# VectorE in place of GpSimd in the planned parts of a two-layer diffusion step, and the recurrence's constants computed first

## The chip, the cores and the metric

One core of a Trainium2 chip runs the whole program in one launch. The metric is the device time of that launch in microseconds (us). The engines are TensorE (PE, with its weight loads as PEld), VectorE (DVE), ScalarE (ACT), GpSimd (POOL) and SyncE (SP, which here only issues DMAs). Each takes its own instructions strictly in program order; an engine waits for another, or for a DMA, at semaphores.

## The reference

640 tokens (128 of a prompt, 512 of a denoising sample, in one array with features on the partitions) pass through two layers and a final norm:

```python
def trunk(x, cvec, ctx_caches):
    for layer in range(DEPTH):                       # DEPTH = 2
        sh_m, sc_m, gt_m, sh_f, sc_f, gt_f = ada_params(cvec, w_mod[layer], b_mod[layer])
        h = rmsnorm(x, g_mix[layer]) * (1.0 + sc_m) + sh_m
        mix = attn_lru_mixer(h, ...) if layer == 0 else pool_mixer(h, w_pool, s_pool)
        x = x + gt_m * mix
        h = rmsnorm(x, g_ffn[layer]) * (1.0 + sc_f) + sh_f
        x = x + gt_f * peer_ffn(h, ...)
    return rmsnorm(x, g_final), new_state
```

`ada_params` is silu(c) @ w_mod + b_mod. `attn_lru_mixer` is latent attention beside a bidirectional RG-LRU recurrence, whose decay is exp(-8 r softplus(-lam)). `pool_mixer` takes centred window means of widths 2 to 16. `peer_ffn` finds for each token and head the 16 best of 128x128 product keys, gathers those experts' rows and sums them. All is float32.

## The kernel before

A float32 product is made from three passes of TensorE over rounded parts: ACT writes the rounded half (`hh` of an activation, `wh` of a weight), another engine writes the rest (`hl`, `wl`) as a subtraction, and PE multiplies hh by wh, hl by wh and hh by wl. So each normed feature block k (8 of them, 128x640) needs, after the RECIPROCAL of the root mean square, a product with `rt` (L483, `xn`), a scale and shift per trunk (L494 on DVE or L491 on ACT), a rounding on ACT (L498), and the rest (L501). Each weight tile needs L307 on ACT and L316 on DVE or POOL.

The program runs in stages:

- The first plan (span 0 to 80 us): modulation columns of layer 0 (weights streamed by DMA; products L1771 on PE; dot products L1802 on DVE, each 128x1024 with its sum, or L1806 on POOL and the sum on ACT, L1810), the first norm, and the first three chunks of the input projection (L529). Behind it `lru_columns` makes the recurrence's column constants from `lam` (L552 to L565: two activations on ACT and 28 operations of 128x8 on DVE).
- The recurrence's plan (80 to 209), the attention's with the output projection (209 to 376).
- Layer 0's PEER: its norm and first query products are planned (from 377); then top-16 searches (L1202 to L1206 on DVE: ten instructions' worth for each of 16 rows of scores in a chunk) and the gather loops, which are written out by hand.
- Layer 1's pooling mixer (planned, 2021 to 2076), its PEER (norm planned from 2079), and the final norm (planned, from 3724).

A `Plan` is a list of operations with their dependencies and, for each engine that could run them, a time (`dve_pool(n)` gives V or G for an elementwise operation of n columns). `run` tries several hundred orderings of the list with those times, puts each operation on the engine where it ends soonest, and then emits the instructions in the best order found. So the tables set both the engine and the place in each engine's queue. `run(S=1.5)` says that ACT is taken for the first 1.5 us. `take` names a ring of buffers that an operation needs. Outside the plans nothing is chosen: there 11 weight rests of each PEER layer (L316) are on POOL, and so are the indirect DMA gathers.

Of the kernel before, what the change touches and what calls it, by code (L numbers as in the profile page):

```python
# [11 lines left out]
F32 = mybir.dt.float32  # L12
# [144 lines left out]
def tile_trunk(ctx: ExitStack, tc: tile.TileContext, a, o):  # L157
# [35 lines left out]
    def mod_ops(plan, l, chunks, pool, tmp, late=0.0):  # L193
        done, loads = {}, []
        prev = []
        for n in chunks:
            w = {}

            def load(e, n=n, w=w):
                w[0] = tmp.tile([128, D], F32, name="wm", tag="wm", bufs=2)  # L200
                SP.dma_start(w[0], a[f"w_mod{l}"][n if l else n - 8])

            ld = plan.add({"SP": 0.1}, load, *loads[-1:], take="wm", late=late)
            arrive = plan.add({"dma": 1.5}, lambda e: None, ld)
            loads.append(ld)
            ends = []
            for cc in range(2):
                pr = {}

                def mult(e, n=n, cc=cc, w=w, pr=pr):  # L210
                    if e is V:
                        junk = tmp.tile([128, D], F16, name="mjunk", tag="mjunk", bufs=1)
                        V.scalar_tensor_tensor(junk, w[0], 1.0, silu[:, cc], op0=OP.mult, op1=OP.mult,
                                               accum_out=mcol[:, l, n, cc:cc + 1])
                    else:
                        pr[0] = pool.tile([128, D], F32, name="mp", tag="mp", bufs=1)
                        G.tensor_tensor(pr[0], w[0], silu[:, cc], op=OP.mult)

                def total(e, n=n, cc=cc, pr=pr):
                    if e is S:  # L220
                        S.activation(pr[0], pr[0], AF.Copy, accum_out=mcol[:, l, n, cc:cc + 1])
# [6 lines left out]
                ends.append(t)  # L228
            done[n] = ends
        return done  # L230
# [92 lines left out]
    class Weights:  # L323
# [143 lines left out]
    def dve_pool(n):  # L467
        return {"V": 0.07 + n * 1.04e-3, "G": 0.1 + n * 2.2e-3}

    def norm_ops(plan, tmp, A, B, rdy, cols_rdy, fine=0):  # L470
# [4 lines left out]
        for k in range(KD):  # L475
            t, xs, hs, ends = [], [], [], []
            for c0, c1 in ((0, HT), (HT, T)) if k < fine else ((0, T),):
# [29 lines left out]
                ends.append(plan.add(dve_pool(c1 - c0), rest, r))  # L507
# [59 lines left out]
    def mixer0(p_mm, tmp, gt, firsts):  # L567
# [6 lines left out]
        with tc.tile_pool(name="pz", bufs=1) as pz:  # L574
# [5 lines left out]
            with tc.tile_pool(name="pa", bufs=1) as pa:  # L580
# [7 lines left out]
                with tc.tile_pool(name="plru", bufs=1) as pl:  # L588
# [76 lines left out]
                    def recurrence(d, jj, prev):  # L665
# [10 lines left out]
                        for q in range(2):  # L676
# [53 lines left out]
                            gm = plan.add(dve_pool(T), gated, sg[1])  # L730
                            rs = plan.add({"V": 1.5}, rest, de, take="t", free=(len(plan.ops),))
                            ro = plan.add({"S": 0.65}, root, rs, table="sqrt")
                            sd = plan.add(dve_pool(T), scaled, ro, gm)
                            en = plan.add({"V": 1.05}, scan, sd)
                            if d:
                                en = plan.add(dve_pool(T), both, en)
# [82 lines left out]
                    for j in range(3):  # L819
                        def scaled(e, j=j):  # L820
                            V.scalar_tensor_tensor(cq[:, j], cq[:, j], col("g_q", j), rtq[0],
                                                   op0=OP.mult, op1=OP.mult)
                        n = plan.add({"V": 0.75}, scaled, rq)
                        h = plan.add({"S": 0.65}, lambda e, j=j: S.activation(hh[:, j], cq[:, j], AF.Copy),
                                     n, ops[0])
                        split.append(plan.add(dve_pool(T), lambda e, j=j: e.tensor_tensor(
                            hl[:, j], cq[:, j], hh[:, j], op=OP.subtract), h))
                    kvn = []
                    for j in range(2):
# [7 lines left out]
                        plan.add(dve_pool(NK), lambda e, j=j: e.tensor_tensor(  # L837
# [12 lines left out]
                    for jj in range(2):  # L850
                        for d in range(2):
                            end = recurrence(d, jj, end)
                        for q in range(2):
                            j = 2 * jj + q
                            plan.add(dve_pool(T), lambda e, j=j, jj=jj, q=q: e.tensor_tensor(
                                gug[:, j], gug[:, j], hss[jj][:, q], op=OP.mult), *end, gugd[j])
                    mod_ops(plan, 0, range(16, 24), None, tmp, 1.0)
# [5 lines left out]
                with tc.tile_pool(name="pv_", bufs=1) as pvp, tc.tile_pool(name="ps", bufs=1) as pS:  # L863
# [3 lines left out]
                    plan = Plan(mm=3, s=2, t=4, mp=1, wm=2)  # L867
# [48 lines left out]
                    for j in range(4):  # L916
                        h = plan.add({"S": 0.65}, lambda e, j=j: S.activation(hh[:, 4 + j], gug[:, j],
                                                                              AF.Copy), *ms, late=1.0)
                        gugs.append(plan.add(dve_pool(T), lambda e, j=j: e.tensor_tensor(
# [124 lines left out]
                    done = mod_ops(plan, 0, range(24, 48), pS, tmp)  # L1044
# [16 lines left out]
                    def sum_up(e):  # L1061
                        ssq.accum()
# [6 lines left out]
                    for d in range(KD):  # L1069
# [10 lines left out]
                        if d < KD - 2:  # L1080
                            parts.append(plan.add({"G": 1.5}, sum_up, q, free=(q,)))
# [12 lines left out]
    def mixer1(p_mm, tmp, A, B, gt):  # L1094
        with tc.tile_pool(name="pq", bufs=1) as pq:
# [53 lines left out]
            for k in (7, 6, 5, 4, 3, 2, 1, 0):  # L1149
# [3 lines left out]
                dep = plan.add(dve_pool(T), tt(xt, xT[:, k], rt, OP.mult), *rdy)  # L1153
                dep = plan.add({"S": 1.1}, hidden(k, xt), dep)
                cur, c0, c1 = hp[:, k], 1, HW
                for lev in range(g + 1):
# [7 lines left out]
                    dep = plan.add(dve_pool(HW), f, dep)  # L1164
                    cur = nx
                dep = plan.add({"V": 0.3, "G": 0.6}, edges(cur, g), dep)
                dep = plan.add({"V": 0.9}, centre(k, cur, xt), dep)
                dep = plan.add({"S": 0.8}, lambda e, k=k, xt=xt: S.activation(hh[:, k], xt, AF.Copy), dep)
                split[k] = plan.add(dve_pool(T), tt(hl[:, k], xt, hh[:, k], OP.subtract), dep)
# [503 lines left out]
    with tc.tile_pool(name="tmp", bufs=1) as tmp, tc.tile_pool(name="pmm", bufs=1, space=PSUM) as p_mm:  # L1673
        with tc.tile_pool(name="pm0", bufs=1) as pm0:
            gb, bb = col("g_mix0"), pm0.tile([128, KD], F32, name="bb")
            A, B, gt = mcol[:, 0, 8:16], mcol[:, 0, 0:8], mcol[:, 0, 16:24]
            plan = Plan(t=4, s=2, sq=4, mp=2, wmn=6, wm=6)
# [59 lines left out]
            for k in range(KD):  # L1737
# [12 lines left out]
                if 0 < k < KD - 2:  # L1750
                    sums = [plan.add(dve_pool(T), join, *prev, *sums, free=prev)]
# [13 lines left out]
            for n in range(8):  # L1765
# [30 lines left out]
                for cc in range(2):  # L1796
                    pr = []

                    def mult(e, n=n, cc=cc, pr=pr):
                        if e is V:  # L1800
                            junk = pm0.tile([128, D], F16, name="mjunk", tag="mjunk", bufs=1)
                            V.scalar_tensor_tensor(junk, scale_w[n], 1.0, silu[:, cc], op0=OP.mult,  # L1802
                                                   op1=OP.mult, accum_out=mcol[:, 0, n + 8, cc:cc + 1])
                        else:
                            pr.append(pm0.tile([128, D], F32, name="mp", tag="mp", bufs=2))
                            G.tensor_tensor(pr[0], scale_w[n], silu[:, cc], op=OP.mult)  # L1806

                    def total(e, n=n, cc=cc, pr=pr):
                        if e is S:
                            S.activation(pr[0], pr[0], AF.Copy, accum_out=mcol[:, 0, n + 8, cc:cc + 1])  # L1810

                    m = plan.add({"V": 1.2, "G": 2.4}, mult, sc_d[n][0], *sl[2 * cc:2 * cc + 2], take=("mp", "G"),
                                 free=(sc_d[n][1],) if cc else ())
                    parts.append(plan.add({"S": 0.95}, total, m, free=(m,), skip=(m, "V")))
# [14 lines left out]
            plan.run(S=1.5)  # L1829
            lru_columns(pm0)  # L1830
        mixer0(p_mm, tmp, gt, firsts)
# [8 lines left out]
    with tc.tile_pool(name="tmp", bufs=1) as tmp, tc.tile_pool(name="pmm", bufs=1, space=PSUM) as p_mm:  # L1840
        plan = Plan()
        rdy = reciprocals(plan)
        for k in range(KD):
            for h in range(2):
                y = []

                def product(e, y=y, k=k, c0=h * HT, c1=h * HT + HT):
                    y.append(tmp.tile([128, HT], F32, name="y", tag="y", bufs=16))
                    if e is V:
                        V.scalar_tensor_tensor(y[0], xT[:, k, c0:c1], col("g_final", k), rt[:, c0:c1],  # L1850
                                               op0=OP.mult, op1=OP.mult)
                    else:
                        G.tensor_tensor(y[0], xT[:, k, c0:c1], rt[:, c0:c1], op=OP.mult)

                def scaled(e, y=y, k=k):
                    if e is S:
                        S.activation(y[0], y[0], AF.Copy, scale=col("g_final", k))
# [110 lines left out]
```

## Time and profile before

| | |
|---|---|
| median of 3 runs | 3744.69 us (3743.12 to 3746.17) |
| profiled execution | 3744.72 us, its span 3743.0 us |
| busy share of the span | PE 96%, PEld 80%, DVE 80%, ACT 44%, POOL 22% |
| chain that ended last | PE 40%, DVE 5%, all others under 1% |
| mean granted clock of PE | 0.979 of full speed |

The shares are means over stages with different limits, so stages are read one by one. In the section with rows, a timeline row gives the start, the duration, engine, line, operation, tiles and shape, the count x of like instructions in a row, and in brackets how long the engine was idle before it and who ended that. A group row of the lines view gives line, engine, operation, shapes and count, then the busy time and the mean in ns of one. A row of the waits view gives who waited for whom: us in total, times, longest. A row of the windows view gives the window, its length, and the busy us and instruction count of PE, PEld, DVE, ACT and POOL, the granted clock of PE, the DMA share and GB/s. Durations of successive DVE instructions overlap by some 0.08 us, so the spacing of starts is the time that one costs.

### The profile page before, as it was taken

What the parts mean: (1) busy time and instruction counts of PE and PEld (TensorE: products, weight loads), DVE (VectorE), ACT (ScalarE), POOL (GpSimd) and SP (SyncE); (2) the same over time, 40 slices, a digit from 0 to 9 for tenths busy, and PEclk for the clock granted to TensorE, in tenths of its full rate; (3) what the DMA queues carried; (4) which work ended last, traced back from release to release, by engine and by line L of the source; (5) the groups of instructions that cost most, each with busy time, mean ns of one, the idle gap of its engine ahead of it and who ended that gap; (6) DMA issues with size and microseconds to landing.
All of it is one profiled execution on the core that took longest, in us unless ns stands there. A gap on an engine that the chain in (4) does not pass through costs nothing. (4 is left out here: it accounts for less than half of the span.)

```text
span 3743.0 us, 52891 instructions
## 1 busy us (share of the span) xinstructions
PE 3589.5 (96%) x18190; PEld 2984.0 (80%) x18190; DVE 2996.6 (80%) x6901; ACT 1645.0 (44%) x2900; POOL 836.7 (22%) x673
## 2 busy tenths in 40 slices
PE   7989889999999999999996798999999999999997
PEld 5957788888888888888885797888888888888886
DVE  7877788898988788888887798988989666666665
ACT  3743323756657333333333323657567433333333
POOL 3122311111111422222223320111211312222221
PEclk9999899999999999999998899999999999999998
DMA  5234125888888999999991215878888978988883
GB/s 200 75 110 141 51 65 196 277 264 287 260 264 283 369 311 327 330 330 324 324 320 47 71 57 172 266 261 287 260 271 278 341 257 296 296 296 297 298 297 105
DMA packets 400162, 894.58 MB, mean 239 GB/s; under 512 B 33746, under 2 KB 170386, under 8 KB 399252
## 3 DMA queue, kind: packets, MB, share of 16 engines
q1 hardware_dynamic: 272884, 490.07, 41.0%
q0 software_dynamic: 74016, 271.09, 21.2%
q10 hardware_dynamic: 52992, 130.05, 8.9%
q8 instruction: 142, 2.33, 0.3%
q14 instruction: 128, 1.05, 0.1%
HBM read 758.26 MB, written 132.81 MB: 238 GB/s over the span
## 5 line engine op out<-in xcount | busy, mean ns | idle before, releaser
L316 DVE TENSOR_TENSOR wl<-wr,wh 128x1024 fp32r<-128x1024 f32 x544 | 660.0, 1214 | 517.6 <-ACT wh L307 440.1
L307 ACT ACTIVATE wh<-wr 128x1024 fp32r<-128x1024 f32 (+1 forms) x578 | 601.5, 1042 | 898.4 <-PE po L1631 735.6
L1287 POOL DMA_INDIRECT gat<-in_u_dram,idx x256 | 292.5, 1143 | 1252.8 <-DVE oh L1477 643.3
L1287 POOL DMA_INDIRECT gat<-in_v_dram,idx x256 | 302.7, 1182 | 1019.1 <-DVE accP L1609 957.5
L1631 PE MATMUL po<-wgh,wh 128*128 128x512 f32 x2032 | 501.8, 389 | 0.0
L1631 PE MATMUL po<-wgl,wh 128*128 128x512 f32 x2032 | 501.8, 389 | 0.0
L1631 PE MATMUL po<-wgh,wl 128*128 128x512 f32 x2032 | 501.8, 389 | 0.0
L1631 PEld LDWEIGHTS po<-wgh,wh 128*128 128x128 f32 x2032 | 381.4, 188 | 79.2
L1631 PEld LDWEIGHTS po<-wgl,wh 128*128 128x128 f32 x2032 | 381.4, 188 | 79.2
L1631 PEld LDWEIGHTS po<-wgh,wl 128*128 128x128 f32 x2032 | 381.4, 188 | 79.2
L1410 DVE SCALAR_TENSOR_TENSOR gat<-gat,hP 128x1024 f32<-128x1024 f32 x256 | 310.8, 1218 | 19.9 <-DMA gat<-in_u_dram,idx 19.8
L1609 DVE SCALAR_TENSOR_TENSOR accP<-gat,aP,accP 128x1024 f32<-128x1024 f32 x254 | 324.8, 1279 | 0.5
L1479 DVE TENSOR_SCALAR oh<-iota,ij,gs 128x128 f16<-128x128 f16 x1024 | 320.0, 313 | 0.0
L1418 ACT ACTIVATE oh<-oh,gs 128x128 f16<-128x128 f16 x1024 | 316.8, 387 | 0.0
L1541 ACT ACTIVATE wgh<-w 128x512 fp32r<-128x512 f32 x256 | 161.9, 632 | 207.7 <-PE po L1631 204.4
L1477 DVE TENSOR_SCALAR oh<-iota,ij 128x128 f16<-128x128 f16 x1024 | 251.4, 246 | 0.0
L1543 DVE TENSOR_TENSOR wgl<-w,wgh 128x512 fp32r<-128x512 f32 x256 | 174.8, 683 | 7.8 <-ACT wgh L1541 7.8
L1430 ACT ACTIVATE stag<-pgm 128x512 f32<-128x512 f32 x256 | 135.5, 579 | 0.0
L316 POOL TENSOR_TENSOR wl<-wr,wh 128x1024 fp32r<-128x1024 f32 (+2 forms) x34 | 72.7, 2138 | 276.4 <-ACT wh L307 276.4
L1423 PE MATMUL pgm<-oh 128*128 128x128 f16 x1024 | 129.4, 220 | 0.0
L1424 PE MATMUL pgm<-oh 128*128 128x128 f16 x1024 | 128.1, 219 | 0.0
L189 DVE SCALAR_TENSOR_TENSOR mjunk<-wm,silu 128x1024 f16<-128x1024 f32 x96 | 116.9, 1218 | 12.7 <-DMA gt__12588<-g_d 9.2
(2282 smaller groups left out, 7223.7 us busy)
## 6 DMA issues: line engine op xcount, KB each, us to landing
wr<-in_uT_dram SPq DMA_DIRECT2D x256, 512.0 KB
wr<-in_v_dram SPq DMA_DIRECT2D x256, 512.0 KB
g_d<-stag ACTq DMA_DIRECT2D x128, 512.0 KB
act_d<-at ACTq DMA_DIRECT2D x240, 256.0 KB
at<-act_d SPq DMA_DIRECT2D x240, 256.0 KB
wm<-in_w_mod_dram SPq DMA_DIRECT2D x88, 512.0 KB
hl<-g_d SPq DMA_DIRECT2D x128, 256.0 KB
wr<-in_w_q_dram SPq DMA_DIRECT2D x32, 512.0 KB
```

The lines of the kernel that those rows point to most:

```text
L307: S.activation(hi[:, :n], RAW[i][:, :n], AF.Copy)
L316: (eng or (V if e == "v" else G)).tensor_tensor(lo[:, :n], RAW.pop(i)[:, :n], hi[:, :n], op=OP.subtract)
L1287: G.indirect_dma_start(out=r, out_offset=None, in_=a[f"u{l}" if s < 128 else f"v{l}"], in_offset=bass.IndirectOffsetOnAxis(ap=idx[:, s % 1 ...
L1410: V.scalar_tensor_tensor(ug, ug, 1.0, hP, op0=OP.mult, op1=OP.mult, accum_out=aP[:, s:s + 1])
L1418: S.activation(oh[:, 2], oh[:, 1], AF.Copy, scale=gr[:, tl:tl + 1])
L1430: S.activation(sg[:, :, t4:t4 + 4], pgm.rearrange("p q i -> p i q"), AF.Copy, scale=1.0 / GSCALE)
L1477: V.tensor_scalar(oh[:, 0], iota16, ij[:, 1, tl:tl + 1], None, op0=OP.is_equal)
L1479: V.tensor_scalar(oh[:, 1], iota16, ij[:, 0, tl:tl + 1], gs[:, 0, tl:tl + 1], op0=OP.is_equal, op1=OP.mult)
L1541: S.activation(wh, w32, AF.Copy)
L1543: return lambda: V.tensor_tensor(wl, w32, wh, op=OP.subtract)
L1609: V.scalar_tensor_tensor(accP, vg, aP[:, s:s + 1], accP, op0=OP.mult, op1=OP.add)
L1631: PE.matmul(po[d], (hi, lo)[x][:, d * 128:(d + 1) * 128], (wh, wl)[y], start=(n == 0 and p == 0), stop=False)
```

## The change

In every plan the POOL choice is taken out: weight rests (L316), both elementwise steps of the norms (L483, L501), the recurrence's products, the sums of squares, the pooling mixer's window sums, the modulation's dot products (with them the sums on ACT) and the final product. DVE is then the only engine for these. `lru_columns` is called ahead of the first plan, which starts with ACT taken for 4.5 us and DVE for 6.0 us. The gathers and the 22 unplanned weight rests stay on POOL.

```diff
-                m = plan.add({"V": 1.2, "G": 2.4} if pool else {"V": 1.2}, mult, arrive, *prev,
-                             take="mp" if pool else None, free=(ld,) if cc else (), late=late)
-                t = plan.add({"S": 0.95}, total, m, free=(m,), late=late,
-                             skip=(m, "V")) if pool else m
+                m = plan.add({"V": 1.2}, mult, arrive, *prev, free=(ld,) if cc else (), late=late)
...
-            self.lo[i] = self.plan.add({"V": 0.1 + n * 1.04e-3, "G": 0.1 + n * 2.2e-3},
+            self.lo[i] = self.plan.add({"V": 0.1 + n * 1.04e-3},
                                        lambda e: (w_lo(i, e), len(RAW) < 3 and w_load()), h)
...
-    def dve_pool(n):
-        return {"V": 0.07 + n * 1.04e-3, "G": 0.1 + n * 2.2e-3}
+    def dve(n):
+        return {"V": 0.07 + n * 1.04e-3}
...
-                x = plan.add(dve_pool(c1 - c0), scale, *deps, *xs[:1], take=None if xs else "t")
+                x = plan.add(dve(c1 - c0), scale, *deps, *xs[:1], take=None if xs else "t")
...
-                            parts.append(plan.add({"G": 1.5}, sum_up, q, free=(q,)))
+                            parts.append(plan.add(dve(T), sum_up, q, free=(q,)))
...
-                    dep = plan.add(dve_pool(HW), f, dep)
+                    dep = plan.add(dve(HW), f, dep)
...
-            plan.run(S=1.5)
             lru_columns(pm0)
+            plan.run(S=4.5, V=6.0)
...
-                m = plan.add({"V": 0.42, "G": 0.85}, product, *rdy[h])
-                t = plan.add({"S": 0.4}, scaled, m, skip=(m, "V"))
+                t = plan.add({"V": 0.42}, product, *rdy[h])
```

Every other site changes in the same way (`dve_pool` to `dve`). Lines move up by 13 or so in the changed kernel: L316 becomes L303, L483 becomes L470, L494 becomes L481, L501 becomes L488, L1802 becomes L1786.

On POOL, in the first plan, these rows stand between the constants at the program's start and the small memsets of the recurrence (`wl` and the second `wm` are weight rests, `mp` a modulation product, `xn` and `hl` the two steps of the norm):

```order
L316 TENSOR_TENSOR wl<-wr,wh 128x1024
L1806 TENSOR_TENSOR mp<-wm,silu 128x1024
L483 TENSOR_TENSOR xn<-xT,rt 128x640 x2
L501 TENSOR_TENSOR hl<-xn,hh 128x640 x2
L483 TENSOR_TENSOR xn<-xT,rt 128x640 x2
L316 TENSOR_TENSOR wm<-wr,wm 128x1024
L1806 TENSOR_TENSOR mp<-wm,silu 128x1024
L501 TENSOR_TENSOR hl<-xn,hh 128x640
L483 TENSOR_TENSOR xn<-xT,rt 128x640
L501 TENSOR_TENSOR hl<-xn,hh 128x640
L483 TENSOR_TENSOR xn<-xT,rt 128x640
L501 TENSOR_TENSOR hl<-xn,hh 128x640
```

In the changed kernel none of these 15 operations is on POOL; all stand in DVE's queue. There the head of the program reads, behind the first instruction `bb` and 27 of the 28 operations of `lru_columns`:

```order
L552 TENSOR_SCALAR s_79<-s_79 128x8
L1730 TENSOR_TENSOR rt<-rt,sq 128x640 x5
L1786 SCALAR_TENSOR_TENSOR mjunk,mcol<-wm,silu 128x1024 x2
L1749 RECIPROCAL rt<-rt 128x320
L1786 SCALAR_TENSOR_TENSOR mjunk,mcol<-wm,silu 128x1024
L1793 TENSOR_SCALAR mcol<-mcol,bb,cols 128x2
L1786 SCALAR_TENSOR_TENSOR mjunk,mcol<-wm,silu 128x1024
L303 TENSOR_TENSOR wl<-wr,wh 128x1024
L1793 TENSOR_SCALAR mcol<-mcol,bb,cols 128x2
L1749 RECIPROCAL rt<-rt 128x320
```

Before, the sums of squares (`rt<-rt,sq`) were DVE's second row, and L552 to L565 its last of this stage, 28 rows behind the last weight rests. Of the eight scale-and-shift pairs of this stage seven were on DVE; now one is, and seven are on ACT. In this plan and in the others an operation's place in the queue moves too, since the search starts from other times.

At the start of layer 0's PEER, DVE's queue before, from the reciprocals of the norm to the middle of the block list:

```order
L441 RECIPROCAL rt<-rt 128x320 x2
L316 TENSOR_TENSOR wl<-wr,wh 128x1024
L483 TENSOR_TENSOR xn<-xT,rt 128x640
L494 TENSOR_SCALAR xn<-xn,mcol 128x320
L494 TENSOR_SCALAR xn<-xn,mcol 128x128
L494 TENSOR_SCALAR xn<-xn,mcol 128x512
L483 TENSOR_TENSOR xn<-xT,rt 128x640
L494 TENSOR_SCALAR xn<-xn,mcol 128x128
L494 TENSOR_SCALAR xn<-xn,mcol 128x512
L501 TENSOR_TENSOR hl<-xn,hh 128x640
```

and in the changed kernel the end of that list, up to the first MAX of the top-16 search:

```order
L481 TENSOR_SCALAR xn<-xn,mcol 128x128
L481 TENSOR_SCALAR xn<-xn,mcol 128x512
L470 TENSOR_TENSOR xn<-xT,rt 128x640
L488 TENSOR_TENSOR hl<-xn,hh 128x640 x2
L303 TENSOR_TENSOR wx_2995<-wr,wx_2994 128x1024
L488 TENSOR_TENSOR hl<-xn,hh 128x640
L303 TENSOR_TENSOR wx_2999<-wr,wx_2998 128x1024
L303 TENSOR_TENSOR wx_2997<-wr,wx_2996 128x1024
L1189 MAX v_2984<-s_3182 128x8
```

The three rests of the later query weights (`wx`), which POOL made before (two of them during the first top-16 searches), now stand on DVE ahead of that search; six scale-and-shift pairs on DVE have become three; and four half-width and three full rests `hl`, four half-width products `xn` and a `wl` have come over from POOL.

## Rows read from the trace of the kernel before

**Rows 1.** Timeline of DVE, first plan.

```profile
25.57 3.06 DVE L494 TENSOR_SCALAR xn<-xn,mcol 128x128 f32<-128x128 f32 x2
28.56 1.21 DVE L1802 SCALAR_TENSOR_TENSOR mjunk<-wm,silu 128x1024 f16<-128x1024 f32 x1
...
29.81 2.44 DVE L1802 SCALAR_TENSOR_TENSOR mjunk<-wm,silu 128x1024 f16<-128x1024 f32 x1
...
32.60 0.80 DVE L494 TENSOR_SCALAR xn<-xn,mcol 128x128 f32<-128x128 f32 x2
33.32 0.82 DVE L483 TENSOR_TENSOR xn<-xT,rt 128x640 f32<-128x640 f32 x1
```

**Rows 2.** Timeline of POOL, first plan.

```profile
29.48 1.68 POOL L501 TENSOR_TENSOR hl<-xn,hh 128x640 fp32r<-128x640 f32 x1 [1.13 <-ACT hh L498]
```

**Rows 3.** DVE's groups by line and shape, window 0 to 80.

```profile
L1802 DVE SCALAR_TENSOR_TENSOR mjunk<-wm,silu 128x1024 f16<-128x1024 f32 x12 | 22.7, 1892 | 0.2
L1817 DVE TENSOR_SCALAR mcol<-mcol,bb,cols 128x2 f32<-128x2 f32 x8 | 8.8, 1102 | 0.0
```

**Rows 4.** Timeline of all engines, end of the first plan.

```profile
61.08 0.28 DVE L1817 TENSOR_SCALAR mcol<-mcol,bb,cols 128x2 f32<-128x2 f32 x1
...
69.10 0.82 DVE L501 TENSOR_TENSOR hl<-xn,hh 128x640 fp32r<-128x640 f32 x1 [0.81 <-ACT hh L498]
...
72.70 1.28 ACT L553 ACT_TABLE_LOAD   x1
...
74.23 0.17 DVE L554 TENSOR_SCALAR ls<-lz 128x8 f32<-128x8 f32 x1 [0.21 <-ACT lz L553]
...
79.40 0.28 ACT L618 ACTIVATE uxp<-pp 128x128 f32<-128x128 f32 x1 [5.20 <-issue]
```

**Rows 5.** Windows: end of the first plan; then the plans named by their times.

```profile
75.00:80.00 5.00, 2.87 (x20) 2.61 (x18) 3.77 (x24) 0.60 (x3) 0.27 (x6) 1.00 0.43 170
...
80.00:209.00 129.00, 122.15 (x731) 112.54 (x732) 114.54 (x146) 93.47 (x132) 23.96 (x19) 0.98 0.28 85
209.00:376.00 167.00, 158.80 (x751) 113.72 (x752) 117.67 (x216) 64.23 (x127) 39.76 (x19) 0.98 0.41 137
...
2021.00:2076.00 55.00, 24.72 (x120) 21.08 (x120) 52.52 (x75) 23.92 (x43) 39.19 (x35) 0.72 0.14 43
```

**Rows 6.** DVE's groups by line and shape, window 377 to 434.

```profile
L483 DVE TENSOR_TENSOR xn<-xT,rt 128x640 f32<-128x640 f32 x6 | 7.4, 1226 | 0.0
L494 DVE TENSOR_SCALAR xn<-xn,mcol 128x512 f32<-128x512 f32 x6 | 5.9, 977 | 0.0
L494 DVE TENSOR_SCALAR xn<-xn,mcol 128x128 f32<-128x128 f32 x6 | 5.4, 893 | 0.2
```

**Rows 7.** Timeline of DVE, start of layer 0's PEER.

```profile
410.71 0.29 DVE L1202 MAX8 v<-s 128x8 f32<-128x128 f32 x1 [5.40 <-ACT s L1348]
...
433.45 0.29 DVE L1202 MAX8 v<-s 128x8 f32<-128x128 f32 x1 [5.59 <-ACT s L1348]
```

**Rows 8.** Waits, window 520 to 560.

```profile
PE pu__4613 L374 <- DVE wl L316: 9.8, 1, 9.8
```

**Rows 9.** Timeline of DVE, then of POOL, start of the pooling mixer.

```profile
2025.81 7.05 DVE L1114 TENSOR_TENSOR xt<-xT,rt 128x640 f32<-128x640 f32 x4
2025.86 8.40 POOL L1114 TENSOR_TENSOR xt<-xT,rt 128x640 f32<-128x640 f32 x4 [3.17 <-DVE rt L441]
```

**Rows 10.** Timeline of DVE, layer 1's PEER.

```profile
2086.48 3.09 DVE L494 TENSOR_SCALAR xn<-xn,mcol 128x128 f32<-128x128 f32 x2
...
2113.09 0.29 DVE L1202 MAX8 v<-s 128x8 f32<-128x128 f32 x1 [6.50 <-ACT s L1348]
...
2135.38 0.29 DVE L1202 MAX8 v<-s 128x8 f32<-128x128 f32 x1 [5.14 <-ACT s L1348]
```

**Rows 11.** Timeline of DVE, final norm.

```profile
3726.15 4.41 DVE L1850 SCALAR_TENSOR_TENSOR y<-xT,cols,rt 128x320 f32<-128x320 f32 x4
...
3732.65 4.17 DVE L1850 SCALAR_TENSOR_TENSOR y<-xT,cols,rt 128x320 f32<-128x320 f32 x6
```

More of the change, by code (lines that the diff above doesn't have):

```diff
@@ L191, in mod_chunks, with mod_ops @@
                 yield 1.15
-    def mod_ops(plan, l, chunks, pool, tmp, late=0.0):
+    def mod_ops(plan, l, chunks, tmp, late=0.0):
         done, loads = {}, []
@@ L503, in norm_ops @@
                 deps = rdy[1 if c0 else 0] + (rdy[1] if c1 == T else [])
-                x = plan.add(dve_pool(c1 - c0), scale, *deps, *xs[:1], take=None if xs else "t")
+                x = plan.add(dve(c1 - c0), scale, *deps, *xs[:1], take=None if xs else "t")
                 h = plan.add({"V": 0.7 * f, "S": 0.2 + 0.95 * f}, affine, x, *cols_rdy(k))
                 r = plan.add({"S": 0.2 + 0.45 * f}, rounded, h)
-                ends.append(plan.add(dve_pool(c1 - c0), rest, r))
+                ends.append(plan.add(dve(c1 - c0), rest, r))
                 xs.append(x)
@@ L729, in recurrence @@
                             de = plan.add({"S": 1.4}, decay, sg[0], table="exp")
-                            gm = plan.add(dve_pool(T), gated, sg[1])
+                            gm = plan.add(dve(T), gated, sg[1])
                             rs = plan.add({"V": 1.5}, rest, de, take="t", free=(len(plan.ops),))
                             ro = plan.add({"S": 0.65}, root, rs, table="sqrt")
-                            sd = plan.add(dve_pool(T), scaled, ro, gm)
+                            sd = plan.add(dve(T), scaled, ro, gm)
                             en = plan.add({"V": 1.05}, scan, sd)
                             if d:
-                                en = plan.add(dve_pool(T), both, en)
+                                en = plan.add(dve(T), both, en)
                             ends.append(en)
@@ L825, in mixer0 @@
                                      n, ops[0])
-                        split.append(plan.add(dve_pool(T), lambda e, j=j: e.tensor_tensor(
+                        split.append(plan.add(dve(T), lambda e, j=j: e.tensor_tensor(
                             hl[:, j], cq[:, j], hh[:, j], op=OP.subtract), h))
@@ L836, in mixer0 @@
                                      kvn[-1], ops[1])
-                        plan.add(dve_pool(NK), lambda e, j=j: e.tensor_tensor(
+                        plan.add(dve(NK), lambda e, j=j: e.tensor_tensor(
                             kvl[:, j], kv[:, j], kvh[:, j], op=OP.subtract), h)
@@ L854, in mixer0 @@
                             j = 2 * jj + q
-                            plan.add(dve_pool(T), lambda e, j=j, jj=jj, q=q: e.tensor_tensor(
+                            plan.add(dve(T), lambda e, j=j, jj=jj, q=q: e.tensor_tensor(
                                 gug[:, j], gug[:, j], hss[jj][:, q], op=OP.mult), *end, gugd[j])
-                    mod_ops(plan, 0, range(16, 24), None, tmp, 1.0)
+                    mod_ops(plan, 0, range(16, 24), tmp, 1.0)
                     for j in range(2):
@@ L866, in mixer0 @@
                     NK2 = NK // 2
-                    plan = Plan(mm=3, s=2, t=4, mp=1, wm=2)
+                    plan = Plan(mm=3, s=2, t=4, wm=2)
                     wts = Weights(plan)
@@ L918, in mixer0 @@
                                                                               AF.Copy), *ms, late=1.0)
-                        gugs.append(plan.add(dve_pool(T), lambda e, j=j: e.tensor_tensor(
+                        gugs.append(plan.add(dve(T), lambda e, j=j: e.tensor_tensor(
                             hl[:, 4 + j], gug[:, j], hh[:, 4 + j], op=OP.subtract), h, late=1.0))
@@ L1043, in mixer0 @@
                             outs.append(plan.add({"V": 0.65 * f}, rest, hi, free=(at,)))
-                    done = mod_ops(plan, 0, range(24, 48), pS, tmp)
+                    done = mod_ops(plan, 0, range(24, 48), tmp)
                     gate = plan.add({"V": 0.1}, lambda e: mod_finish(0, 16, 24))
@@ L1152, in mixer1 @@
                 sw = [pq.tile([128, HW], F32, name=f"sw{k}_{n}") for n in range(min(g + 1, 2))]
-                dep = plan.add(dve_pool(T), tt(xt, xT[:, k], rt, OP.mult), *rdy)
+                dep = plan.add(dve(T), tt(xt, xT[:, k], rt, OP.mult), *rdy)
                 dep = plan.add({"S": 1.1}, hidden(k, xt), dep)
@@ L1163, in mixer1 @@
                         f = tt(nx[:, c0:c1], cur[:, c0 - w:c1 - w], cur[:, c0 + w:c1 + w], OP.add)
[L1164 removed]
+                    dep = plan.add(dve(HW), f, dep)
                     cur = nx
[L1166 removed]
+                dep = plan.add({"V": 0.3}, edges(cur, g), dep)
                 dep = plan.add({"V": 0.9}, centre(k, cur, xt), dep)
                 dep = plan.add({"S": 0.8}, lambda e, k=k, xt=xt: S.activation(hh[:, k], xt, AF.Copy), dep)
[L1169 removed]
+                split[k] = plan.add(dve(T), tt(hl[:, k], xt, hh[:, k], OP.subtract), dep)
                 tiles = {k: xt} if k % 2 else {**tiles, k: xt}
@@ L1676, in tile_trunk @@
             A, B, gt = mcol[:, 0, 8:16], mcol[:, 0, 0:8], mcol[:, 0, 16:24]
-            plan = Plan(t=4, s=2, sq=4, mp=2, wmn=6, wm=6)
+            plan = Plan(t=4, s=2, sq=4, wmn=6, wm=6)
             queue, bus = [], []
@@ L1750, in tile_trunk @@
                 if 0 < k < KD - 2:
-                    sums = [plan.add(dve_pool(T), join, *prev, *sums, free=prev)]
+                    sums = [plan.add(dve(T), join, *prev, *sums, free=prev)]
                 elif k == 0:
@@ L1796, in tile_trunk, with mult @@
                 for cc in range(2):
[L1797 to L1814, printed above, removed]
+                    def mult(e, n=n, cc=cc):
+                        junk = pm0.tile([128, D], F16, name="mjunk", tag="mjunk", bufs=1)
+                        V.scalar_tensor_tensor(junk, scale_w[n], 1.0, silu[:, cc], op0=OP.mult,
+                                               op1=OP.mult, accum_out=mcol[:, 0, n + 8, cc:cc + 1])
+                    parts.append(plan.add({"V": 1.2}, mult, sc_d[n][0], *sl[2 * cc:2 * cc + 2],
+                                          free=(sc_d[n][1],) if cc else ()))
                 def scale_end(e, n=n):
```

30 lines of the change are left out of this document (8 added, 22 removed).

## The prediction

> **What bounds the kernel now.** The table of busy shares says PE (96%), but that is a mean over stages, and the change touches only the planned ones. I therefore read the windows first, to find the plans in which PE starves, then the timelines of DVE and POOL there, to see what one operation costs alone and beside the other engine, and last the waits behind them. In the recurrence's and the attention's plans PE is busy for 122 of 129 and 159 of 167 us, so little is to be had; in the pooling mixer PE is busy for 25 of 55 us and DVE for 52.5: DVE is the bound [rows 5]. It is the bound too in the first plan, from the root to the last `hl`, and at the start of both PEERs.
>
> What is to be seen in those timelines is that DVE and POOL don't add up. The same dot product of 128x1024 takes 1.21 us at 28.56 and 2.44 at 29.81 [rows 1]; the second began while POOL was in a rest that ran from 29.48 to 31.16, so 1.35 of it were left [rows 2], and the dot product is 1.23 longer. A scale-and-shift pair takes 0.80 alone and 3.06 at 25.57 [rows 1]. Four products of 640 columns on each engine, started together, take DVE 7.05 and POOL 8.40 [rows 9]; alone, one costs DVE 0.74 (0.82 listed, less 0.08 of overlap [rows 1]), so all eight would have been done in 5.9. The Trainium skill ("SBUF — State Buffer", "SBUF: two separate sides") says that the second port pair is an exclusive lock between GpSimd and a VectorE operation with two SBUF inputs or in a two-port mode, and that the later one waits for the whole instruction; the row at 29.81 agrees (1.23 against 1.35).
>
> **The change, stage by stage.** In each I take what DVE gets back (contended mean less the duration alone) and add what it takes over.
>
> *First plan.* Back: twelve dot products, 22.7 - 12 x 1.21 = 8.2; eight column steps of 128x2, 8.8 - 8 x 0.28 = 6.6 (0.28 alone [rows 4]) [rows 3]; one pair 2.3 [rows 1]: 17.1. Taken over, by the count on POOL: 11 of 640 columns x 0.74 = 8.1, and four of 1024 at 1.2 = 4.9: 13.0. Six pairs go to ACT, 6 x 0.72 = 4.3 less. The constants at the head cost 5.2 there (74.23 to 79.40 [rows 4]), where DVE waits for inputs and ACT's squares anyway; what I charge is the extra table load on ACT in front of the squares, 1.3 (1.28 [rows 4]). Sum -17.1 + 13.0 - 4.3 + 1.3 = -7.1: the last `hl`, at 69.92 [rows 4], comes at about 62.8. Behind it the two weight rests and the constants kept DVE until 79.4, and ACT's first evacuation for the recurrence started at 79.40, when the constants were done [rows 4], although PE had run out at about 77.9 (2.87 of the last 5 us [rows 5]). That is 9.5 us behind the last `hl`. With the constants gone, PE's remaining products set this: 8.0 (77.9 - 69.9) if the backlog is as long as now, 4 if PE has kept up. So the stage ends at 66.8 to 70.8 in place of 79.4: -12.6 to -8.6. Bounds with the unknown rest: -15 and -8. I take **-12**, near the lower bound, since the change also frees ACT of two sums and PE's waits were for `hl`. If that cover is wrong (PE half-clocked and late) the value is -8.
>
> *Recurrence and attention.* DVE is busy 114.5 of 129 and 117.7 of 167, POOL 24.0 and 39.8 [rows 5]. At 0.74 for 1.7 (POOL's rest of 640 columns took 1.68 [rows 2]), the 24.0 become 10.4 on DVE; what comes back is at most 24.0 and at least nothing: +10 to -14 on an engine with 14 us of idle, which PE's 122 us cover but for 7. I take **-3** (-6 to +3). In the attention PE's cover is 159 of 167: **0** (-3 to +4); a weight rest that now queues behind dot products could cost PE a few us there.
>
> *Layer 0's PEER start.* Back: six products 7.4 - 6 x 0.82 = 2.5, six pairs 5.9 + 5.4 - 6 x 0.80 = 6.5 [rows 6]: 9.0. Taken over ahead of the last `hl`: two weight rests 2.4, three rests of 640 at 0.74, eight halves at 0.4: 7.8. Three pairs fewer, -2.2. So the last `hl` comes 3.4 to 5 earlier. Behind it DVE waits 5.40 for the first scores; two weight rests (2.4) stand there now and hide in that wait. Then DVE searches two chunks without a gap and waits 5.59 again at 433.45 for the third chunk's scores [rows 7]; POOL made that chunk's weight rests (`wx`) during the first searches, and in the new order they are ready before them, so the third chunk's products can move up and this wait should go. From there DVE sets the pace: later PE waits 9.8 us for a weight rest that stands behind searches [rows 8], so what DVE gains here reaches the end. -3.4 - 5.6 = **-9** (-4 if the second wait stays, -12 if contended operations without a row here add 3).
>
> *Pooling mixer.* DVE takes over POOL's 39.2 us of 35 operations [rows 5]. By the four beside four [rows 9], 8.40 of POOL become 4 x 0.74 = 3.0 on DVE: 14.0. Back: there 7.05 - 3.0 = 4.1 for 8.40, 0.48 for each us of POOL, which would be 18.9 if every us collided, 9 if half did. I take 13: **+1** (-5 to +5).
>
> *Layer 1's PEER start.* As in layer 0 with fewer operations from POOL (three `wx`, two rests, three half products: 3.6 + 1.5 + 1.2 = 6.3, two thirds of it ahead of the last `hl`), pairs to ACT -2.2, and stalls of which one pair shows 3.09 - 0.80 = 2.3 [rows 10], some 5 in all if the others are like it: -3. Waits of 6.50 and 5.14 before the first and the third search [rows 10]; the second may go. **-7** (-3 to -11).
>
> *Final norm.* Ten products in 4.41 + 4.17 = 8.6, with six on POOL [rows 11]; sixteen on DVE at 0.42 (half of 0.82) are 6.7: **-2**.
>
> *PEER loops.* Same order, 11 unplanned rests of each layer stay on POOL: 0.
>
> Sum: -12 - 3 + 0 - 9 + 1 - 7 - 2 = -32. The profiled execution took 3744.72, 0.03 over the median; so **3713**.
>
> **Rivals.** (1) *DVE becomes the bound*: what stretches DVE's operations is not POOL, or POOL's work really ran beside it. For it: DVE is the fullest engine in these stages. Against it: the 2.44 beside 1.21, and eight operations in 8.40 that DVE alone does in 5.9. Place: pooling mixer +14, first plan +3 (13.0 - 4.3 + 1.3, less the 5.2 of the constants and their wait), layer 0's PEER +5, layer 1's +4, final +2, recurrence +5: +33, 3778. In the sum above about 17 + 9 + 13 + 5 + 4 = 48 us come back; below a third of that the change is slower. The Trainium skill ("Perfetto Trace Analysis", "Optimizing Scalar/DVE Operations") has both: with a saturated VectorE, moving work to ScalarE or even GpSimd may pay, which speaks against this change, and between those two it might not help, as they share a read port. The rows bear out the second. Chance 0.05.
> (2) *Half the gain*: PE, at a lower clock where it starves, and its backlog set the starts of the stages; -8 in the first plan, -4 and -3 in the PEERs (both second waits stay), -3 for the rest: -18, 3727. For it: PE's 8.0 of products behind the last `hl`, and the granted clock of 0.72 in the pooling mixer, a mean of the levels of 1.2 and 2.4 GHz in a stretch where PE was busy for 25 of 55 us [rows 5]. Chance 0.2.
> (3) *Every us of POOL was lost to DVE*: the lower bounds together, -15 - 6 - 3 - 12 - 5 - 11 - 2 = -54, 3691. Against it: in the first plan 17 us come back by rows where POOL works some 28 (eleven of 640 columns at 1.68, four of 1.6 times the columns). Chance 0.08. The lock of the Trainium skill ("SBUF — State Buffer", "SBUF: two separate sides"), if every instruction of POOL met a waiting one of DVE, would give this.
> (4) *Given back*: the next plan's weights and the PE-bound recurrence swallow the first plan's gain, and the searches their own: within 7 us of before. Against it: the loads of the recurrence are issued behind the same weight rests, which come earlier too. Chance 0.05.
>
> **How the numbers follow.** The forecast has 0.62. Its own bounds, 10 to 12 us either way for stages that err independently, with (2) inside, give 3698 to 3731; that leaves out (1), (3) and (4). 0.2% are 7.5 us, about what a measurement of this kernel can tell from no change: faster 0.91, the same 0.05, slower 0.04.
>
> **What would show it.** Right: dot products and column steps at 1.2 and 0.28 throughout; the recurrence's first evacuation at 66 to 71; the last `hl` of layer 0's PEER some 4 us nearer to its root, no 5.6 us wait at the third chunk; the pooling mixer as long as before (54 to 58). Wrong: DVE operations that stay long with POOL idle; PE still in the first plan's products after 72; long waits of PE for weight rests in the attention.

## The result, and the profile after

The changed kernel took 3703.64 us (median of 4 runs, 3699.02 to 3704.95) against 3743.9 for the kernel before on the same chip: ratio 0.9888, 95% interval 0.9876 to 0.99, 40 us less. The profiled execution has a span of 3703.2. On its page:

```profile
span 3703.2 us, 52825 instructions
PE 3581.9 (97%) x18190; PEld 2980.4 (80%) x18190; DVE 2976.3 (80%) x6989; ACT 1644.4 (44%) x2904; POOL 656.2 (18%) x564
```

DVE has 88 instructions more than before and is busy for 20 us less. The groups of DVE by line and shape in the first plan show why; they answer to [rows 3]:

```profile
L1786 DVE SCALAR_TENSOR_TENSOR mjunk<-wm,silu 128x1024 f16<-128x1024 f32 x16 | 19.5, 1218 | 0.8 <-ACT silu L1717 0.5
...
L1793 DVE TENSOR_SCALAR mcol<-mcol,bb,cols 128x2 f32<-128x2 f32 x8 | 2.3, 285 | 0.1
```

The sixteen dot products take 1.218 us on the mean (twelve took 1.892), and a column step 0.285 in place of 1.102. At the start of layer 0's PEER the same is to be seen (window 357 to 385; beside [rows 6], where these shapes took 1226 and 977 ns):

```profile
L470 DVE TENSOR_TENSOR xn<-xT,rt 128x640 f32<-128x640 f32 x6 | 4.9, 818 | 0.0
...
L481 DVE TENSOR_SCALAR xn<-xn,mcol 128x512 f32<-128x512 f32 x2 | 1.1, 540 | 0.0
```

The timelines of DVE, ACT and PE at the end of the first plan, which answer to [rows 4]:

```profile
59.82 0.82 DVE L488 TENSOR_TENSOR hl<-xn,hh 128x640 fp32r<-128x640 f32 x1 [0.80 <-ACT hh L485]
62.40 2.36 DVE L303 TENSOR_TENSOR wl<-wr,wh 128x1024 fp32r<-128x1024 f32 x2 [1.75 <-ACT wh L294]
...
63.22 0.26 ACT L605 ACTIVATE uxp<-pp 128x128 f32<-128x128 f32 x1
...
75.12 4.54 PE L672 MATMUL pg<-xT,wg 128*128 128x320 f32 x16 [3.00 <-DMA wm<-in_w_mod_dram]
```

The last `hl` comes 9.3 us earlier, and the recurrence's first evacuation (ACT's copy of PE's first sums, `uxp<-pp`) 16.2 earlier (63.22 for 79.40). Further on, DVE at the starts of layer 0's PEER, of the pooling mixer, of layer 1's PEER and in the final norm (to be read beside [rows 7, 10, 11]):

```profile
358.22 2.15 DVE L428 RECIPROCAL rt<-rt 128x320 f32<-128x320 f32 x1 [2.77 <-ACT rt L421]
...
384.88 0.29 DVE L1189 MAX8 v<-s 128x8 f32<-128x128 f32 x1 [1.37 <-ACT s L1335]
...
406.30 0.29 DVE L1189 MAX8 v<-s 128x8 f32<-128x128 f32 x1 [4.28 <-ACT s L1335]
...
1994.89 4.16 DVE L428 RECIPROCAL rt<-rt 128x320 f32<-128x320 f32 x2 [1.10 <-ACT rt L421]
...
2056.02 2.15 DVE L428 RECIPROCAL rt<-rt 128x320 f32<-128x320 f32 x1 [2.37 <-ACT rt L421]
...
2080.34 0.29 DVE L1189 MAX8 v<-s 128x8 f32<-128x128 f32 x1 [2.79 <-ACT s L1335]
...
2099.54 0.29 DVE L1189 MAX8 v<-s 128x8 f32<-128x128 f32 x1 [2.03 <-ACT s L1335]
...
3688.06 2.15 DVE L428 RECIPROCAL rt<-rt 128x320 f32<-128x320 f32 x1 [1.56 <-ACT rt L421]
...
3696.24 3.79 DVE L1825 SCALAR_TENSOR_TENSOR y<-xT,cols,rt 128x320 f32<-128x320 f32 x8
```

The first reciprocal of each norm, called its root below, is a landmark that both traces have (before: 377.37, 2021.62, 2079.60 and 3723.86). Subtracting them splits the 39.8 us of the span:

| from | to | before | after | difference | forecast |
|---|---|---|---|---|---|
| start | first evacuation of the recurrence | 79.40 | 63.22 | -16.2 | -12 |
| evacuation | root, layer 0's PEER | 297.97 | 295.00 | -3.0 | -3 |
| that root | root, pooling mixer | 1644.25 | 1636.67 | -7.6 | -9 |
| that root | root, layer 1's PEER | 57.98 | 61.13 | +3.2 | +1 |
| that root | root, final norm | 1644.26 | 1632.04 | -12.2 | -7 |
| that root | end of the span | 19.14 | 15.14 | -4.0 | -2 |

### The profile page after: what moved, and what is told of

Read it like the earlier page. It is cut to its first block, busy times and chain, and to the rows that moved or that the text cites. A ratio compares the mean times of both kernels' runs of the same rounds, so it can differ in the third digit from the quotient of the medians.

```text
span 3703.2 us, 52825 instructions
## 1 busy us (share of the span) xinstructions
PE 3581.9 (97%) x18190; PEld 2980.4 (80%) x18190; DVE 2976.3 (80%) x6989; ACT 1644.4 (44%) x2904; POOL 656.2 (18%) x564
## 5 line engine op out<-in xcount | busy, mean ns | idle before, releaser
L303 DVE TENSOR_TENSOR wl<-wr,wh 128x1024 fp32r<-128x1024 f32 (+2 forms) x556 | 665.7, 1198 | 518.7 <-ACT wh L294 448.3
L1410 PEld LDWEIGHTS <-oh 128*128 128x128 f16 x1024 | 96.9, 98 | 33.5 <-DVE oh L1464 23.3
```

The costliest lines, as they stand in the source:

```text
L303: (eng or (V if e == "v" else G)).tensor_tensor(lo[:, :n], RAW.pop(i)[:, :n], hi[:, :n], op=OP.subtract)
L1410: PE.matmul(pgm[:, n], oh[:, 0], oh[:, 1], start=True, stop=False)
```

## The experiments

Each kernel below was timed against the kernel before on its own chip; stage lengths are from its profile. Two profiles of one order of work can differ by some us in the attention (below), so small effects are read from stages.

**Work for POOL that nobody needs.** The theory of the prediction is that a POOL operation shuts DVE's operations out. Its rival is that the planner's new order, with the pairs on ACT, made the gain. Extra products on POOL, in the changed kernel, leave the order of the other engines as it is:

```diff
+            dum = pm0.tile([128, T], F32, name="dum")
...
+            def root(e, h):
+                V.reciprocal(rt[:, h * HT:(h + 1) * HT], rt[:, h * HT:(h + 1) * HT])
+                for i in range(12 if h else 0):
+                    G.tensor_tensor(dum, rt, xT[:, 0], op=OP.mult)
...
```

> The changed kernel with twelve products of 128x640 added on POOL (into a tile that nobody reads), released by the second reciprocal of the first norm; the order on PE, DVE, ACT and SP is unchanged. Theory 1 (a POOL operation that reads SBUF shuts VectorE's operations out while it lasts): DVE's dot products and column steps stretch again to 2.4 and 1.3 to 2.3 us, twelve times 0.8 to 1.6 us come on top, the last hl moves from 59.8 to 70 to 79, and the time from 3703.6 to 3712 to 3721. Theory 2 (the gain came from the planner's new order and from ACT taking the affine pairs, not from POOL's silence): DVE's durations stay at 1.22 and 0.28, and the time stays at 3703.6 within 2.

Measured 3727.13, ratio 0.9944 (0.9929 to 0.9959): 23 us over the changed kernel, more than either theory had. DVE's timeline tells why:

```profile
26.71 2.55 DVE L303 TENSOR_TENSOR wl<-wr,wh 128x1024 fp32r<-128x1024 f32 x1
...
29.18 1.50 DVE L1799 TENSOR_SCALAR mcol<-mcol,bb,cols 128x2 f32<-128x2 f32 x1
45.18 2.15 DVE L1752 RECIPROCAL rt<-rt 128x320 f32<-128x320 f32 x1 [14.50 <-POOL dum L1754]
```

The products read `rt`, whose other half the next reciprocal had still to write, so DVE stood 14.5 us for them: an ordinary wait for a buffer, not the port. The run decides nothing but for the two stretched rows ahead of that wait (2.55 for 1.22, 1.50 for 0.28). So it was made again with products that read `silu` and `xT`, behind one half-size product:

```diff
...
+                if h:
+                    G.tensor_tensor(dum[:, :HT], rt[:, HT:], xT[:, 0, :HT], op=OP.mult)
+                    for i in range(12):
+                        G.tensor_tensor(dum, silu[:, 0, :T], xT[:, 0], op=OP.mult)
...
```

> The first run with added products held DVE's second reciprocal back for 14.5 us, because the products read the tile that it writes; its price is not that of the port. Here the twelve added products of 128x640 on POOL read two tiles that nobody writes in this stage; one half-size product ahead of them waits for the first reciprocal. Theory 1 (POOL's operations shut VectorE's out): the operations of DVE between 23 and about 50 us stretch as in the kernel before, 8 to 19 us in sum; the last hl moves from 59.8 to 66 to 76; time 3710 to 3721. Theory 2 (order and placement alone made the gain): durations 1.22 and 0.28, last hl at 59.8, time 3703.6 within 3.

Measured 3718.86, ratio 0.9932 (0.9915 to 0.9949): 15 us over the changed kernel. Timelines of POOL and of DVE:

```profile
25.48 26.37 POOL L1756 TENSOR_TENSOR dum<-silu,xT 128x640 f32<-128x640 f32 x12
```

```profile
30.37 2.14 DVE L1752 RECIPROCAL rt<-rt 128x320 f32<-128x320 f32 x1
32.54 3.87 DVE L470 TENSOR_TENSOR xn<-xT,rt 128x640 f32<-128x640 f32 x2
36.34 2.55 DVE L1794 SCALAR_TENSOR_TENSOR mjunk<-wm,silu 128x1024 f16<-128x1024 f32 x1
...
50.39 1.48 DVE L1801 TENSOR_SCALAR mcol<-mcol,bb,cols 128x2 f32<-128x2 f32 x1
51.79 0.81 DVE L488 TENSOR_TENSOR hl<-xn,hh 128x640 fp32r<-128x640 f32 x1
52.52 1.21 DVE L1794 SCALAR_TENSOR_TENSOR mjunk<-wm,silu 128x1024 f16<-128x1024 f32 x1
...
74.61 0.82 DVE L488 TENSOR_TENSOR hl<-xn,hh 128x640 fp32r<-128x640 f32 x1 [0.80 <-ACT hh L485]
```

While POOL works (25.48 to 51.85), two products take 3.87 in place of 1.56, a dot product 2.55 in place of 1.22, a column step 1.48 in place of 0.28; the reciprocal keeps its 2.14. From 51.8 on everything is as in the changed kernel. The last `hl` moves by 14.8 us, on an unchanged order. The rival falls for this stage: POOL's work itself is the cost, 14.8 us of DVE for twelve products and the half-size one, and with POOL busy the new order's last `hl` (74.61) is even later than that of the kernel before (69.10). DVE would have made these products itself in 9.3 us (0.74 each, 0.4 for the half). In the other stages POOL was not loaded again in this way; there the explanation rests on the durations read from the traces.

**The same with memsets**, so that POOL writes but reads nothing:

```diff
-                        G.tensor_tensor(dum, silu[:, 0, :T], xT[:, 0], op=OP.mult)
+                        G.memset(dum, 0.0)
```

(24 of them in place of the 12 products.)

> The same, with 24 memsets of 128x640 in place of the twelve products: POOL writes, but reads nothing. If only a POOL operation that reads SBUF shuts out DVE's operations with two inputs, the dot products and rests stay at 1.22 and 0.82 and only the one-input column steps and pairs may stretch: last hl at 60 to 63, time 3703 to 3707. If any POOL operation does it: as with the products, 3708 and more.

Measured 3705.62, ratio 0.9888 (0.9871 to 0.9904), as the changed kernel. POOL's timeline, then DVE's:

```profile
25.39 16.49 POOL L1756 MEMSET dum<- 128x640 f32 x24
```

```profile
26.41 1.21 DVE L303 TENSOR_TENSOR wl<-wr,wh 128x1024 fp32r<-128x1024 f32 x1
27.55 0.56 DVE L1801 TENSOR_SCALAR mcol<-mcol,bb,cols 128x2 f32<-128x2 f32 x1
...
29.92 1.56 DVE L470 TENSOR_TENSOR xn<-xT,rt 128x640 f32<-128x640 f32 x2
...
60.70 0.82 DVE L488 TENSOR_TENSOR hl<-xn,hh 128x640 fp32r<-128x640 f32 x1 [0.80 <-ACT hh L485]
```

Beside 16.5 us of memsets the operations with two inputs in SBUF keep their 1.21 and 1.56; only the column steps, with one tile as input, grow, to 0.56 at 27.55 and 0.77 at 37.69. This is the distinction of the Trainium skill ("SBUF — State Buffer", "SBUF: two separate sides"): VectorE operations with two SBUF inputs collide only with a GpSimd operation that reads SBUF, those in a two-port mode with any; the rows with two inputs agree with it (1.21 and 1.56 kept). That the column step runs in such a mode is not shown by a row; that it grows fits.

**The two parts of the change apart.** First the changed kernel with the constants back behind the first plan:

```diff
-            lru_columns(pm0)
-            plan.run(S=4.5, V=6.0)
+            plan.run(S=1.5)
+            lru_columns(pm0)
```

> The changed kernel with the column constants back behind the first plan (POOL still idle in the plans). Theory 1: the constants are worth the 5.2 us of DVE at the end of the first plan plus a wait for the table load, less 1.9 that they cost at the head: 3707 to 3712. Rival: the constants at the head are most of the 15.4 us that the first plan gained, since they held the first evacuation: 3714 to 3720.

Measured 3707.99, ratio 0.9899 (0.9883 to 0.9914), 4 us over the changed kernel by the ratios, with overlapping intervals. Then the kernel before with that edit the other way round, POOL working as before:

```diff
-            plan.run(S=1.5)
             lru_columns(pm0)
+            plan.run(S=4.5, V=6.0)
```

> The kernel before with only the column constants moved ahead and the plan started at ACT 4.5 and DVE 6.0; POOL works as before. Theory 1: -3 to -7 against before (3737 to 3741). Rival: -12 or more, so that the two parts of the change share the first plan's gain the other way round.

Measured 3744.85, ratio 0.9995 (0.9986 to 1.0004): no difference that shows, where theory 1 had 3 to 7 us less. The evacuations of the recurrence, in the timelines of ACT of these two kernels:

```profile
69.91 0.28 ACT L605 ACTIVATE uxp<-pp 128x128 f32<-128x128 f32 x1 [5.22 <-issue]
```

```profile
74.74 0.26 ACT L618 ACTIVATE uxp<-pp 128x128 f32<-128x128 f32 x1
```

So the constants are worth 6.7 us at the end of the first plan with POOL out (69.91 to 63.22) and 4.7 with POOL in (79.40 to 74.74), as expected. At the root of layer 0's PEER the first pair of kernels is only 1.0 apart (359.21 and 358.22), and the second 3.5 (377.37 and 373.89); the time of the second pair shows nothing of that, and where it went was not tried. In the first pair the loss lies behind the attention's first scores: from the evacuation to there both kernels take 130 us, although the changed one waits 3.00 for the gate weights (75.12 in its rows above). What differs from there on is TensorE's clock. Windows of the changed kernel, and of the one with the constants late, at the first scores of the attention (same order on PE, seven us apart):

```profile
200.00:205.00 5.00, 4.02 (x9) 1.75 (x10) 3.47 (x9) 2.94 (x5) 0.00 (x0) 0.81 0.86 237
205.00:210.00 5.00, 5.00 (x13) 2.44 (x11) 1.76 (x6) 0.96 (x3) 0.00 (x0) 0.50 0.06 20
210.00:215.00 5.00, 5.00 (x23) 4.52 (x23) 3.47 (x10) 2.86 (x7) 0.00 (x0) 0.67 0.00 0
```

```profile
207.00:212.00 5.00, 3.65 (x11) 1.39 (x11) 3.47 (x10) 2.94 (x5) 0.00 (x0) 1.00 0.76 246
212.00:217.00 5.00, 5.00 (x26) 3.85 (x27) 4.21 (x12) 3.05 (x9) 0.00 (x0) 1.00 0.10 39
```

In the one the granted clock goes from 1.00 to 0.50 (1.2 of 2.4 GHz) after PE has waited 0.98 us for the softmax, in the other it stays at 1.00 after a wait of 1.35. From the first score to the last this costs 90.9 against 86.7 us. It belongs to the execution and not to the constants: in the profile of the last experiment below, whose instructions up to this root are those of the changed kernel, the clock stays up at the same place, and the root comes at 353.05, 6.2 us before that of the kernel with the constants late.

```profile
200.00:205.00 5.00, 3.27 (x10) 1.18 (x8) 3.52 (x9) 2.93 (x5) 0.00 (x0) 1.00 0.86 261
205.00:210.00 5.00, 5.00 (x24) 3.42 (x24) 4.19 (x12) 2.84 (x9) 0.00 (x0) 1.00 0.15 59
```

```profile
353.05 2.15 DVE L428 RECIPROCAL rt<-rt 128x320 f32<-128x320 f32 x1 [2.77 <-ACT rt L421]
```

**POOL back in the pooling mixer**, the one stage that became longer:

```diff
-                dep = plan.add(dve(T), tt(xt, xT[:, k], rt, OP.mult), *rdy)
+                dep = plan.add(dve_pool(T), tt(xt, xT[:, k], rt, OP.mult), *rdy)
...
-                    dep = plan.add(dve(HW), f, dep)
+                    dep = plan.add(dve_pool(HW), f, dep)
```

(and so the edges, the rests and the weight rests there.)

> The changed kernel with POOL given back to the planner in the pooling mixer alone (products, window sums, edges, rests and its weight rests). In the changed kernel this stage is 3.1 us longer from root to root than before. Theory 1: those come back, 3700.5 within 2, with DVE's sums stretched as before. Rival: the 3.1 us come from the next stage's order or from PE, not from DVE's extra work: 3703.6 or more.

Measured 3708.14, ratio 0.9901 (0.9886 to 0.9917): not faster than the changed kernel, and not the 3700.5 of theory 1. DVE's timeline:

```profile
1997.37 4.17 DVE L430 RECIPROCAL rt<-rt 128x320 f32<-128x320 f32 x2 [1.10 <-ACT rt L423]
...
2055.36 2.15 DVE L430 RECIPROCAL rt<-rt 128x320 f32<-128x320 f32 x1 [1.05 <-ACT rt L423]
...
2081.34 0.29 DVE L1195 MAX8 v<-s 128x8 f32<-128x128 f32 x1 [2.95 <-ACT s L1341]
```

The stage is 58.0 long again, as in the kernel before. But the 3.2 us are not DVE's extra work. Windows of the whole stage in the kernel before, in the changed one and in this one:

```profile
2021.00:2079.00 58.00, 27.46 (x128) 22.52 (x128) 53.83 (x77) 25.35 (x45) 39.45 (x35) 0.74 0.16 48
```

```profile
1995.00:2056.00 61.00, 32.03 (x128) 26.77 (x128) 53.75 (x112) 25.97 (x44) 0.00 (x0) 0.66 0.16 50
```

```profile
1997.40:2055.40 58.00, 27.58 (x128) 22.65 (x128) 53.84 (x78) 25.37 (x44) 39.44 (x35) 0.74 0.16 49
```

DVE takes over 35 operations that kept POOL busy for 39.45 us, and is busy for 53.75 us in place of 53.83: all that it took over came back from its own operations. The stage is longer because DVE stands idle for 7.3 us in place of 4.2. Above all it waits for PE's products in the pooling mixer, 4.6 us in three waits where it was 1.1 in one; PE is busy for 32.0 us in place of 27.5, at a granted clock of 0.66 in place of 0.74. So the rival holds for the stage too, in its second form: the time comes from PE. Whether the new order or the clock makes PE late was not separated. With POOL back, the next stage up to the first search takes 26.0 in place of 24.3.

**DVE in place of POOL beside the searches too**, the 22 unplanned weight rests:

```diff
-        add_seq(f"w_q{l}", 16, 8, 128, "g")
+        add_seq(f"w_q{l}", 16, 8, 128, "v")
```

> The changed kernel with the 11 unplanned weight rests of each PEER layer moved from POOL (2.4 us each) to DVE (1.14), so that POOL does no elementwise work beside the top-16 searches either. Theory: the searches read one tile and were never stretched by POOL, DVE sets the pace there, so up to 22 x 1.14 = 25 us come on top: 3712 to 3729. Rival (POOL's rests hold up the searches as they held up the norms): 3690 to 3700.

Measured 3726.22, ratio 0.9951 (0.9935 to 0.9968): 23 us slower than the changed kernel, within the 25 of the theory. The searches never paid for POOL; the spread of their durations in the kernel before, by line, with its 22 rests of 2.4 us on POOL beside them:

```profile
L1202 DVE MAX8 v<-s x160: 272/274/295, 410.7 to 2254.2; 128x8 f32<-128x128 f32 x160
```

The longest of 160 is 295 ns, and of the 37 that ran beside a rest on POOL it is 278. There the same exchange is a loss: POOL's time was free, and DVE's is not.

**The third chunk's scores earlier**, for the wait of 4.28 us that stayed:

```diff
-                    if c > 2:
+                    if c == 2:
+                        score(2)
+                    elif c > 3:
                         score(c - 1)
```

> The changed kernel with the third chunk's scores issued right behind its products, ahead of the fourth chunk's products. In the changed kernel DVE still waits 4.28 us (layer 0) and 2.03 us (layer 1) for these scores. If they are late because TensorE takes the fourth chunk first, both waits go and the time falls by 4 to 6, to 3697.5 to 3700; if they are late because the third chunk's products are, nothing changes: 3703.6 within 2.

Measured 3702.94, ratio 0.9888 (0.9871 to 0.9904): no change that shows. The wait moved one chunk on, in layer 0 and in layer 1:

```profile
409.84 0.30 DVE L1189 MAX8 v<-s 128x8 f32<-128x128 f32 x1 [5.11 <-ACT s L1335]
...
2102.55 0.30 DVE L1189 MAX8 v<-s 128x8 f32<-128x128 f32 x1 [2.77 <-ACT s L1335]
```

So the third chunk's scores did come sooner, and the fourth chunk's then came late. PE is busy for 28.73 of the 31 us from 379 to 410 in this run, at a clock of 1.00: its products set the pace here, whichever chunk's scores are taken first.

## Why the prediction held, step by step

*What bounds the kernel.* Right. Stretched operations are what DVE got back, and in the first plan, the one stage where this was tried, added work on POOL brings the stretch back on an unchanged order. The durations forecast (1.2 and 0.28 throughout) are in the rows. Of the other signs named, the evacuation came before its 66 to 71, the wait at the third chunk stayed, and the pooling mixer took 61.1 for 54 to 58; none of the signs of being wrong came.

*First plan*: -12 forecast, -16.2 measured, just outside its bounds (-15 to -8). The end of the last `hl` was forecast at 62.8 and came at 60.6: of these 2.2 us, 1.2 are a second scale-and-shift pair that POOL had stretched (2.03 at 52.97, for 0.80) and that was not counted. The table load was charged at 1.3; the first reciprocal comes 1.9 later (21.03 for 19.14). The other 2.0 us are the step that was mis-sized, the stretch behind the last `hl`, for which PE's backlog of 4 to 8 us stood. PE does work on the plan's products for 4.3 us more (to 64.9), but the first evacuation need not wait for all of them: it comes 2.6 us behind, and PE goes from the one plan's products to the next without a gap.

*Recurrence and attention*: -3 and 0 forecast, -3.0 measured; that they agree is luck. Seven of the profiles have the changed kernel's order up to the root of layer 0's PEER. In four of them, the changed kernel's among them, the clock falls at the attention's first scores, and the two stages take 295.0 to 298.0; in three it does not, and they take 289.9 to 291.3, 6.7 to 8.1 less than before. Both lie inside the bounds given (-9 to +7 for the two together). DVE takes over the 64.0 us that POOL worked there and is busy for 232.7 us before (79 to 377) and after (63 to 358); what shrinks is PE's idle time, from 16.6 to 10.7 us. The constants' early start is given back, as rival (4) had it for the whole gain, in the profile in which the clock falls, and mostly kept where it does not.

*Layer 0's PEER*: -9 forecast, -7.6 measured, by two errors that nearly cancel. The first search starts 6.7 us nearer to the root (26.7 us behind it, for 33.3), not 3.4; the last `hl` came 6.1 earlier in its stage (21.8 us behind the root, for 27.9). The step that failed is "this wait should go": the wait at the third chunk is 4.28 for 5.59. It was put down to the place of the weight rests; the run with the scores moved shows that PE's products set the pace there.

*Pooling mixer*: +1 forecast, +3.2 measured, within its bounds (-5 to +5). The sum was of DVE's work, 14 taken over and 13 back, and by the windows it came out at nothing; the 3.2 are waits for PE, which the sum did not have.

*Layer 1's PEER*: -7 forecast, -12.2 measured, just outside its bounds. DVE's list gave 5.5 where 3 stood (from root to the end of the last rest before the search, 27.0 and 21.5). The wait before the first search fell from 6.50 to 2.79, which was not in the sum, and that at the third chunk from 5.14 to 2.03, 3.1 where some 4 stood.

*Final norm*: -2 forecast, -4.0 measured. From the root to the end of DVE's last product it is 1.0 (12.96 and 11.97); 3.0 lie behind it, where the outputs are issued and land. Why that tail is shorter was not tried and stays open.

The sum was -32 and the time -40, inside the range. The mechanism held; the errors of the single stages have both signs, and part of the nearness is that they cancel.

## What to carry to other kernels

Before elementwise work is shared between VectorE and GpSimd, look in the trace for one operation's duration alone and beside the other engine. Where products and subtractions of two SBUF tiles double, an engine that looks idle may have nothing to give: here twelve and a half products on GpSimd cost VectorE 14.8 us, which would make them itself in 9.3, and in the pooling mixer 39.45 us of GpSimd's work went over to VectorE without adding to its busy time. A planner that prices both engines as if they ran side by side will then spread work that costs more than it saves. Where VectorE runs operations that do not stretch (here the searches), the same exchange is a loss of nearly all that it moves (23 of 25 us). And a gain at the end of one stage is compared further on in more than one profile: here 6.7 us of earlier start were 1.0 at the next landmark in a profile in which TensorE's clock fell, and 6.2 in one in which it did not.

## What the runs showed of the hardware

- A GpSimd product of two tiles stretches VectorE's two-input operations (1.22 to 2.55, 0.78 to 1.9 and 2.1) and its column steps (0.28 to 1.5), and takes longer itself (26.37 us for twelve, 2.2 each, where a subtraction of the same size took 1.68 in [rows 2]). A reciprocal of 128x320 keeps its 2.14 beside it, and a MAX8 its 0.27 beside a weight rest.
- GpSimd memsets (0.69 us each) leave the two-input operations alone, and stretch only the column steps (0.28 to 0.77 at the most).
- TensorE's granted clock can fall to 1.2 GHz in one run and stay at 2.4 in another at the same instruction of the same order, after waits of 0.98 and 1.73 us: in the changed kernel it fell at 203 us, in the kernel with the scores moved, whose order up to there is the same, it did not, and the root of layer 0's PEER came at 353.05 in place of 358.22. Of seven profiles of this order it fell there in four, for 10.2 us each. The runs don't show what decides it.
